# Moving the split weights of the 256-column products 64 bytes off a multiple of 256, in a fixed ring of four tiles

## The chip, the cores and the metric

The kernel runs on one core of one Trainium2 chip. The metric is the device time of one execution in microseconds, the median of three: 1817.12 us before the change (1815.8 to 1817.33). The profile is that of a further execution, which took 1815.54 us. TensorE (PE in the profile, its weight loads PEld) does the products, VectorE (DVE), ScalarE (ACT) and GpSimd (POOL) everything else, and SyncE (SP) issues most of the transfers.

## The reference

Two layers of a hybrid block on 512 tokens of 1024 features, in float32. What matters here are its matrix products:

```
h = rms_norm(x);  proj = h @ w_in            # 27 + 24 tiles of 128 columns, + two of 512
y_a = sparse attention (q, k, v, top 128 keys by an index score)
y_b = gated linear recurrence (conv, sigmoid gates, scan)
y_c = u * (w_spatial @ rms_norm(v))          # 8 masked 128x128 matrices
x = x + rms_norm(sum_n sigmoid(gate_n) * (y_n @ w_branch_n) @ w_out)
x = x + rms_norm(relu(rms_norm(x) @ w_up)**2 @ w_down)
x = x + rms_norm((p @ w_ple) * sigmoid(x @ w_ple_gate))
```

## The kernel before

Activations lie with features on the 128 partitions and the 512 tokens along the free dimension. TensorE works in `float32r`; to reach float32 precision every operand is split into a high part (rounded to `float32r`) and a low part (the rest), and each product is made of three: hi by hi, lo by hi, hi by lo (`mm3`, L361 to L363; the same three on one line in `gemm_arriving`, L419). The weight is the stationary operand, 128x128 at a time, and the activation streams past it: 512 columns as a rule, 256 where a stage is cut in two halves of the tokens so that the next norm can begin on the first half. The products of 256 columns are: in `gemm_halves`, the last three tiles of the output projection (`out` 5 to 7) and of the gate (`gate` 5 to 7); in `gemm_arriving`, the first four tiles of the up projection (`up` 0 to 3) and, in the second layer, the first three of the input projection (`xr` 0 to 2); and the spatial gating (`sp`), where the masked weight streams, two blocks of 128 columns at a time, past a stationary activation. The attention has small products of its own (transposes L1046, values L1060, logits L745 and L749), which use no weight.

Weights come in 306 tiles of 128x1024, in the order of a list (`order`). `prep` takes the next one: SP loads it into one of three buffers (`wr`), ACT casts it to the high part (`wh`, L253), DVE subtracts that from it for the low part (`wl`, L254). `getw` hands a weight out and first calls `prep` until it is three weights ahead (`LA`); for a branch weight (`br`) only one ahead. `wh` and `wl` are two tags of a pool with four buffers each (`NWB`). The built program shows which buffer each tile took: the four of a tag are not taken in turn, and each begins at a multiple of 512 bytes of its partition, as do the activations. A branch weight serves two branch products with a gate product between them (`gated`), so it is held longer than the gate weights that are handed out behind it.

[...] In the attention, `turn` transposes a piece of the probabilities into PSUM, splits it with a cast on ACT (L432) and a subtraction on DVE (L433), and `values` (L1060) multiplies both parts: four products, the first two with the high part, the other two with the low one.

Of the kernel before, what the change touches and what calls it, by code (L numbers as in the profile page):

```python
# [9 lines left out]
F32R = mybir.dt.float32r  # L10
# [35 lines left out]
def f32v(ap):  # L46
    return ap.bitcast(F32)
# [3 lines left out]
def hybrid_block_kernel(ctx, tc, xT, pT, pos, vec, bsp, freq, w_in, w_tok, w_lru, w_sp, w_br, w_out, w_up, w_dn, w_ple, w_gate, out, depth=DEPTH, dbg=None):  # L51
# [4 lines left out]
    wp = ctx.enter_context(tc.tile_pool(name="wp", bufs=1))  # L56
# [6 lines left out]
    def nm(p):  # L63
        uid[0] += 1
        return f"{p}_{uid[0]}"

    def tmp(dt=F32):
        return tp.tile([128, S], dt, tag="tmp", name=nm("tmp"), bufs=NTMP)
# [7 lines left out]
    def slot(tag, dt=F32, big=False):  # L76
        return cp.tile([128, 4, S] if big else [128, S], dt, tag=tag, name=nm(tag))
# [8 lines left out]
    NWB = 4  # L86
# [151 lines left out]
    nprep = [0]  # L238
    nget = [0]

    def prep():
        weights_first()
        i = nprep[0]
        nprep[0] += 1
        key, src = order[i]
        raw = wp.tile([128, 1024], F32, tag="wr", name=nm("wr"), bufs=3)
        nc.sync.dma_start(raw, src)
        if key[0] == "sp":
            r3 = raw.rearrange("p (g t) -> p g t", g=8)
            G.affine_select(out=r3, in_=r3, compare_op=ALU.is_ge, fill=0.0, base=0, pattern=[[0, 8], [1, 128]], channel_multiplier=-1)  # L250
        hi = wp.tile([128, 1024], F32R, tag="wh", name=nm("wh"), bufs=NWB)
        lo = wp.tile([128, 1024], F32R, tag="wl", name=nm("wl"), bufs=NWB)
        A.copy(hi, raw)  # L253
        V.tensor_sub(lo, raw, f32v(hi))  # L254
        prepared[key] = (hi, lo)
        if not strict[0]:
            return
        ins = nc.cur_bb.bb.instructions
        parts[:] = [len(ins)] + [next(i.name for i in reversed(ins) if i.engine == e) for e in ENG]
# [5 lines left out]
    def weights_first():  # L265

        if not parts:
            return
        for i in nc.cur_bb.bb.instructions[parts[0]:]:
            for e, name in zip(ENG, parts[1:]):  # L270
                if i.engine == e:
                    tc.add_manual_dep(i, name, mybir.DependencyInfo(mybir.DependencyClass.NoSync, mybir.DependencyReason.SCHED_ONLY), reason="weights first")
        parts.clear()

    def getw(key, ahead=LA):
        assert order[nget[0]][0] == key, (order[nget[0]][0], key)
        nget[0] += 1
        while nprep[0] < min(nget[0] + ahead, len(order)):
            prep()
        return prepared.pop(key)  # L280
# [104 lines left out]
    def gemm_halves(keys, xs, evac, done):  # L385


        ws = [getw(key, LA if i == 0 else 0) for i, key in enumerate(keys)]
        for r in HALVES:
            for i, w in enumerate(ws):  # L390
                ps = bank()[:, :S // 2]
                gemm(ps, w, xs, KT, r=r)
                evac(i, r, ps)
                if r is HALVES[1] and nprep[0] < len(order):
                    prep()
            done(r)

    def gemm_arriving(keys, xs, source, ranges, arrived=None, lag=LAG, tail=TAIL):


        n = len(keys)
        ws = [getw(key, 0) for key in keys[:-1]]
        pss = [bank() for _ in keys]
        last = {}
        for r in ranges:
            gen = source(r)
            for k in range(KT):
                with ordered(last):
                    next(gen)
                    todo = [(o, k) for o in range(len(ws))]  # L410
                    if len(ws) < n and k == lag:
                        ws.append(getw(keys[-1], 0))
                        todo += [(n - 1, q) for q in range(k + 1)]
                    if r is ranges[-1] and k >= KT - tail:
                        todo = [] if k < KT - 1 else [(o, q) for o in range(n) for q in range(KT - tail, KT)]
                    for i, (o, q) in enumerate(todo):
                        h3, l3 = [v.rearrange("p (k c) -> p k c", k=KT) for v in ws[o]]
                        for m in range(3):
                            PE.matmul(pss[o][:, r], (h3, l3, h3)[m][:, q], xs[q][m // 2][:, r], start=q == 0 and m == 0, stop=q == KT - 1 and m == 2)  # L419
                        if r is ranges[-1] and q == KT - 1 and o < n - 1:  # L420
                            prep()
                tick(0.65 * len(todo) * width(r) / S)
            if arrived is not None:
                arrived(r)
        while nprep[0] < nget[0] + LA:
            prep()
        return pss
# [146 lines left out]
    chunks = []  # L574
    for key, src in order[:3]:
        raw = wp.tile([128, 1024], F32, tag="wr", name=nm("wr"), bufs=3)
        hi = wp.tile([128, 1024], F32R, tag="wh", name=nm("wh"), bufs=NWB)
        lo = wp.tile([128, 1024], F32R, tag="wl", name=nm("wl"), bufs=NWB)
        prepared[key] = (hi, lo)
        chunks.append((src, raw, hi, lo))  # L580
    nprep[0] = 3
# [19 lines left out]
    for l in range(depth):  # L601
# [31 lines left out]
        def proj(name, ahead=LA):  # L633
            ps = bank()
            gemm(ps, getw(("in", l, name), ahead), XS, KT)
            return ps
# [12 lines left out]
        def rope(ps, n=128):  # L649
            t1, u = tmp(), tmp()  # L650
            V.tensor_mul(t1[:n], ps[:n], Cr[:n])
            V.stream_shuffle(u[:n], ps[:n], mask=SHUF)
            G.tensor_mul(u[:n], u[:n], Sr[:n])  # L653
            G.tensor_add(t1[:n], t1[:n], u[:n])  # L654
            return t1
# [25 lines left out]
        for j in range(4):  # L681
            ps = first[j]
            xr = tmp()
# [242 lines left out]
        for j in range(4):  # L926
# [7 lines left out]
            r, i = slot(f"B{j}"), tmp()  # L934
# [177 lines left out]
        for j in range(4):  # L1112
            f = rope(proj(f"q{j}"))
# [23 lines left out]
        for d in range(8):  # L1137
# [3 lines left out]
            hi, lo = slot(f"M{d}", F32R), ml[d // 4][:, d % 4]  # L1141
# [196 lines left out]
```

## Time and profile before

| what | value |
|---|---|
| median of three executions | 1817.12 us |
| the profiled execution | 1815.54 us |
| its span | 1813.8 us |
| PE busy | 1789.2 us, 99% |
| DVE, ACT, POOL busy | 63%, 43%, 19% |
| matmuls, each with its weight load | 8748 |

The span is what the profile covers; some 1.7 us of the execution lie around it. PE is busy from end to end at the full granted clock, so what a part costs is read from how far apart its matmuls start, and from the few places where PE waits. The busy time of one matmul row is longer than the distance to the next, because they overlap.

### The profile page before, as it was taken

What the parts mean: (1) busy time and instruction counts of PE and PEld (TensorE: products, weight loads), DVE (VectorE), ACT (ScalarE), POOL (GpSimd) and SP (SyncE); (2) the same over time, 40 slices, a digit from 0 to 9 for tenths busy, and PEclk for the clock granted to TensorE, in tenths of its full rate; (3) what the DMA queues carried; (4) which work ended last, traced back from release to release, by engine and by line L of the source; (5) the groups of instructions that cost most, each with busy time, mean ns of one, the idle gap of its engine ahead of it and who ended that gap; (6) DMA issues with size and microseconds to landing.
All of it is one profiled execution on the core that took longest, in us unless ns stands there. A gap on an engine that the chain in (4) does not pass through costs nothing.

```text
span 1813.8 us, 22748 instructions
## 1 busy us (share of the span) xinstructions
PE 1789.2 (99%) x8748; PEld 1497.5 (83%) x8748; DVE 1149.9 (63%) x1946; ACT 787.3 (43%) x1289; POOL 340.8 (19%) x277
## 2 busy tenths in 40 slices
PE   9999999999999999999999999999999999999997
PEld 7888788888988888888888888788889888888886
DVE  8789987656375254534688899876565743544345
ACT  6547246554443222223546473466534422222233
POOL 0612123200420000002454131332004100000033
PEclk9999999999999999999999999999999999999998
DMA  5312322222222232332222222322222323222321
GB/s 176 105 60 97 105 93 94 70 82 82 93 93 94 95 103 93 96 113 86 91 80 99 69 94 84 114 82 70 82 93 70 105 95 103 93 97 102 105 82 58
DMA packets 49676, 167.75 MB, mean 92 GB/s; under 512 B 6048, under 2 KB 8864, under 8 KB 49568
## 3 DMA queue, kind: packets, MB, share of 16 engines
q1 hardware_dynamic: 47376, 163.64, 27.3%
q10 hardware_dynamic: 2192, 2.67, 0.4%
q8 instruction: 68, 1.11, 0.3%
q14 instruction: 40, 0.33, 0.1%
HBM read 164.19 MB, written 2.10 MB: 92 GB/s over the span
## 4 chain that ended last, share of the span: by engine, by line
PE 75%; DVE 14%; POOL 4%; ACT 4%; issue 3%; DMA 0%; SPq 0%; POOLq 0%; ACTq 0%; DVEq 0%
PE ps L361 22%; PE ps L363 22%; PE ps L362 22%; PE ps L419 4%; DVE wl L254 3%; DVE tmp L794 2%; DVE m L792 2%; PE ps L668 2%; PE ps L1060 1%; POOL tmp L653 1%; ACT wh L253 1%; PE ps L1046 1%; POOL sacc L461 1%; PE ps L759 1%; POOL tmp L654 1%
## 5 line engine op out<-in xcount | busy, mean ns | idle before, releaser
L253 ACT CAST wh<-wr 128x1024 fp32r<-128x1024 f32 x303 | 317.2, 1050 | 476.9 <-PE ps L363 397.1
L254 DVE TENSOR_TENSOR wl<-wr,wh 128x1024 fp32r<-128x1024 f32 x303 | 379.2, 1254 | 199.7 <-ACT wh L253 199.3
L361 PE MATMUL ps<-xh,wh 128*128 128x512 f32 (+1 forms) x1296 | 502.5, 388 | 0.0
L363 PE MATMUL ps<-xl,wh 128*128 128x512 f32 (+1 forms) x1296 | 495.4, 382 | 0.0
L362 PE MATMUL ps<-xh,wl 128*128 128x512 f32 (+1 forms) x1296 | 495.2, 382 | 0.0
L363 PEld LDWEIGHTS ps<-xl,wh 128*128 128x128 f32 x1296 | 243.6, 188 | 47.7
L361 PEld LDWEIGHTS ps<-xh,wh 128*128 128x128 f32 x1296 | 243.8, 188 | 45.7 <-issue 1.9
L362 PEld LDWEIGHTS ps<-xh,wl 128*128 128x128 f32 x1296 | 244.1, 188 | 43.3
L461 POOL TENSOR_TENSOR sacc<-sacc,tmp 128x256 f32<-128x256 f32 (+1 forms) x92 | 98.0, 1065 | 884.6 <-issue 584.5
L363 PE MATMUL ps<-V,wh 128*128 128x512 f32 (+1 forms) x528 | 195.4, 370 | 0.0
L363 PE MATMUL ps<-B,wh 128*128 128x512 f32 x336 | 131.1, 390 | 0.0
L361 PE MATMUL ps<-A,wh 128*128 128x512 f32 x320 | 125.0, 390 | 0.0
L362 PE MATMUL ps<-A,wl 128*128 128x512 f32 x320 | 124.5, 389 | 0.0
L1197 DVE TENSOR_TENSOR M<-M,ps 128x512 f32<-128x512 f32 x48 | 33.0, 688 | 141.3 <-PE ps L363 141.3
L1185 DVE TENSOR_TENSOR tmp<-ps,R 128x512 f32<-128x512 f32 x64 | 43.8, 690 | 112.1 <-PE ps L363 109.5
L363 PEld LDWEIGHTS ps<-V,wh 128*128 128x128 f32 x528 | 99.5, 188 | 16.8
L361 PE MATMUL ps<-K,wh 128*128 128x512 f32 x256 | 99.6, 389 | 0.0
L362 PE MATMUL ps<-K,wl 128*128 128x512 f32 x256 | 99.6, 389 | 0.0
L419 PE MATMUL ps<-xl,wh 128*128 128x256 f32 (+1 forms) x264 | 86.2, 326 | 5.5 <-DVE xl L567 5.1
L419 PE MATMUL ps<-xh,wl 128*128 128x256 f32 (+1 forms) x264 | 84.1, 319 | 0.8 <-DVE wl L254 0.8
L419 PE MATMUL ps<-xh,wh 128*128 128x256 f32 (+1 forms) x264 | 84.5, 320 | 0.1
L363 PEld LDWEIGHTS ps<-B,wh 128*128 128x128 f32 x336 | 63.1, 188 | 13.4
(243 smaller groups left out, 2835.7 us busy)
## 6 DMA issues: line engine op xcount, KB each, us to landing
wr<-in_w_in_dram SPq DMA_DIRECT2D x95, 512.0 KB, 3.3
wr<-in_w_up_dram SPq DMA_DIRECT2D x64, 512.0 KB, 3.2
wr<-in_w_dn_dram SPq DMA_DIRECT2D x64, 512.0 KB, 3.2
wr<-in_w_br_dram SPq DMA_DIRECT2D x24, 512.0 KB, 3.2
wr<-in_w_tok_dram SPq DMA_DIRECT2D x16, 512.0 KB, 3.2
wr<-in_w_out_dram SPq DMA_DIRECT2D x16, 512.0 KB, 3.2
wr<-in_w_gate_dram SPq DMA_DIRECT2D x16, 512.0 KB, 3.2
X<-in_xT_dram SPq DMA_DIRECT2D x8, 256.0 KB, 5.7
```

What stands on the lines that cost most here:

```text
L253: A.copy(hi, raw)
L254: V.tensor_sub(lo, raw, f32v(hi))
L361: PE.matmul(ps, wh, xh, start=start, stop=False)
L362: PE.matmul(ps, wl, xh, start=False, stop=False)
L363: PE.matmul(ps, wh, xl, start=False, stop=stop)
L419: PE.matmul(pss[o][:, r], (h3, l3, h3)[m][:, q], xs[q][m // 2][:, r], start=q == 0 and m == 0, stop=q == KT - 1 and m == 2)
L461: G.tensor_add(sacc[:, r], sacc[:, r], self.q[r.start, r.stop])
L668: PE.matmul(ps, x, w, start=k == 0 and i == 0, stop=k == KT - 1 and i == 2)
L792: V.max(m8, (sc if r == 0 else wk)[:, :n])
L794: V.match_replace(wk[:, :n], m8, (sc if r == 0 else wk)[:, :n], -3.0e38)
L1185: V.tensor_mul(t, ps, R)
L1197: V.tensor_add(F[d], F[d], ps)
```

## The change

`home` takes the place of the two pool tags. There are four tiles with a tag each (`wp0` to `wp3`), taken strictly in turn as weights are recorded, and each holds hi and lo of one weight side by side. The two odd tiles are 2064 elements wide and the even ones 2096, so that in the built program the even ones begin at a multiple of 256 bytes and the odd ones at 192 more. The offset `c` of 16 elements (64 bytes) is set so that the weights named in `narrow` begin 64 or 192 bytes past a multiple of 256 and all others at a multiple of 256 (for two of the four tiles one that is not a multiple of 512). The work arrays behind them lie 512 bytes further on.

```
+    narrow = set()
+    for l in range(depth):
+        narrow.add(("sp", l))
+        narrow.update(("out", l, d) for d in (5, 6, 7))
+        narrow.update(("gate", l, d) for d in (5, 6, 7))
+        narrow.update(("up", l, 0, i) for i in range(4))
+        if l:
+            narrow.update(("in", l, f"xr{j}") for j in range(3))
+    ring = [0]
+
+    def home(key):
+
+        i = ring[0] % NWB
+        ring[0] += 1
+        t = wp.tile([128, 2064 if i % 2 else 2096], F32R, tag=f"wp{i}", name=nm("wp"))
+        c = 16 if (key in narrow) == (i % 2 == 0) else 0
+        return t[:, c:c + 1024], t[:, c + 1024:c + 2048]
...
-        hi = wp.tile([128, 1024], F32R, tag="wh", name=nm("wh"), bufs=NWB)
-        lo = wp.tile([128, 1024], F32R, tag="wl", name=nm("wl"), bufs=NWB)
+        hi, lo = home(key)
         A.copy(hi, raw)
         V.tensor_sub(lo, raw, f32v(hi))
```

The same two lines are replaced where the first three weights are set up. No instruction is removed, and none is added but six loads of an activation table on ACT, three in each layer, where the scheduler sets square roots (L957) and gates' tanh (L919) in turns; SP's loads keep their order. Lines of the kernel after are 17 or 18 higher than before.

What moves is shown at one place, a piece of the first head pair's attention whose values are multiplied while a branch product runs (layer 0). The same is found at a second place of the layer, in the next head pair, and at the same two in layer 1. On ACT before, the cast of the probabilities (`tmp_3092`, L432) stands between the casts of two weights:

```order
L432 CAST tmp_3056<-ps_3051 128x512
L253 CAST wh_3078<-wr_3076 128x1024
L432 CAST tmp_3092<-ps_3088 128x384
L253 CAST wh_3186<-wr_3184 128x1024
L1033 ACTIVATE tmp_3111,mx_3112<-tmp_3111,mx_3112 128x128
```

On ACT after, both weights' casts stand ahead of it (`tmp_3035` is the same piece; `wp_3129` is the branch weight, recorded last, and `wp_3022` the gate weight recorded before it):

```order
L450 CAST tmp_3001<-ps_2996 128x512
L271 CAST wp_3129<-wr_3127 128x1024
L271 CAST wp_3022<-wr_3020 128x1024
L450 CAST tmp_3035<-ps_3031 128x384
L1050 ACTIVATE tmp_3054,mx_3055<-tmp_3054,mx_3055 128x128
```

The two weights have changed places, and the probabilities have moved behind the second. DVE's two subtractions moved likewise, ahead of that of the probabilities (`tmp_3036`). On PE before, at the same place, the values with the high part (`tmp_3092`) stand five products ahead of the branch product's end, those with the low part (`tmp_3093`) at its end:

```order
L361 MATMUL ps_3168<-B_417_1976,wh_2850 128x512
L1060 MATMUL ps_2988<-tmp_3092,V_455_2139 128x256
L1060 MATMUL ps_2988<-tmp_3092,V_455_2139 128x128
L362 MATMUL ps_3168<-B_417_1976,wl_2851 128x512
L363 MATMUL ps_3168<-B_418_1977,wh_2850 128x512
L361 MATMUL ps_3168<-B_428_2038,wh_2850 128x512
L362 MATMUL ps_3168<-B_428_2038,wl_2851 128x512
L363 MATMUL ps_3168<-B_429_2039,wh_2850 128x512
L1060 MATMUL ps_2988<-tmp_3093,V_455_2139 128x256
L1060 MATMUL ps_2988<-tmp_3093,V_455_2139 128x128
L361 MATMUL ps_3183<-xh_12_187,wh_2978 128x512
```

On PE after, all four stand behind the branch product (`ps_3111`), whose weight is `wp_2798`:

```order
L380 MATMUL ps_3111<-B_382_1941,wp_2798 128x512
L381 MATMUL ps_3111<-B_383_1942,wp_2798 128x512
L379 MATMUL ps_3111<-B_392_2002,wp_2798 128x512
L380 MATMUL ps_3111<-B_392_2002,wp_2798 128x512
L381 MATMUL ps_3111<-B_393_2003,wp_2798 128x512
L1077 MATMUL ps_2933<-tmp_3035,V_417_2101 128x256
L1077 MATMUL ps_2933<-tmp_3035,V_417_2101 128x128
L1077 MATMUL ps_2933<-tmp_3036,V_417_2101 128x256
L1077 MATMUL ps_2933<-tmp_3036,V_417_2101 128x128
L379 MATMUL ps_3126<-xh_12_187,wp_2924 128x512
```

The five products that stood between the two pairs of values have moved ahead of both.

## Rows read from the trace of the kernel before

**Rows 1.** The page: busy us (share) xinstructions; granted TensorE clock in 40 slices.
```profile
PE 1789.2 (99%) x8748; PEld 1497.5 (83%) x8748; DVE 1149.9 (63%) x1946; ACT 787.3 (43%) x1289; POOL 340.8 (19%) x277
PEclk9999999999999999999999999999999999999998
```

**Rows 2.** Timeline of PE, out projection of 512 columns: start us, length us.
```profile
451.74 0.39 PE L363 MATMUL ps<-V,wh 128*128 128x512 f32 x1
...
461.94 0.39 PE L363 MATMUL ps<-V,wh 128*128 128x512 f32 x1
```

**Rows 3.** The same a little later, in its halves of 256 columns.
```profile
471.36 0.28 PE L361 MATMUL ps<-M,wh 128*128 128x256 f32 x1
...
477.96 0.28 PE L362 MATMUL ps<-M,wl 128*128 128x256 f32 x1
```

**Rows 4.** Groups of PE by shape, products of 256 columns: count, busy us, mean ns.
```profile
L419 PE MATMUL ps<-xh,wh 128*128 128x256 f32 x176 | 50.2, 285 | 0.0
...
L361 PE MATMUL ps<-M,wh 128*128 128x256 f32 x96 | 27.5, 286 | 0.0
...
L361 PE MATMUL ps<-wh,K 128*128 128x256 f32 x32 | 9.0, 282 | 0.0
```

**Rows 5.** Timeline of PE: four transposes, eight products of 2 columns.
```profile
271.59 0.60 PE L1046 MATMUL ps<-ident,tmp 128*128 128x128 f32 x4
...
845.72 1.05 PE L471 MATMUL ps<-ones,tmp 128*128 128x2 f32 x8
```

**Rows 6.** Groups of PE and PEld by shape: the same kinds, mean ns of one.
```profile
L1046 PE MATMUL ps<-ident,tmp 128*128 128x128 f32 x160 | 26.0, 273 | 0.0
...
L471 PE MATMUL ps<-ones,tmp 128*128 128x2 f32 x24 | 3.3, 254 | 1.5 <-ACT tmp L455 1.5
...
L362 PEld LDWEIGHTS ps<-xh,wl 128*128 128x128 f32 x1296 | 244.1, 188 | 43.3
...
L1046 PEld LDWEIGHTS ps<-ident,tmp 128*128 128x128 f32 x160 | 20.4, 140 | 7.0 <-ACT tmp L1035 0.8
...
L471 PEld LDWEIGHTS ps<-ones,tmp 128*128 128x128 f32 x24 | 3.0, 191 | 2.2 <-ACT tmp L455 2.2
```

**Rows 7.** Waits of PE and of PEld: us in total, times, longest.
```profile
PE ps L419 <- DVE xl L567: 5.1, 10, 0.9
...
PEld ps L1060 <- ACT tmp L432: 1.2, 4, 0.4
```

**Rows 8.** Timeline of ACT at the two places of moved instructions, layer 0.
```profile
328.74 1.05 ACT L253 CAST wh<-wr 128x1024 fp32r<-128x1024 f32 x1 [7.27 <-PE ps L363]
329.69 0.47 ACT L432 CAST tmp<-ps 128x384 fp32r<-128x384 f32 x1
331.90 1.05 ACT L253 CAST wh<-wr 128x1024 fp32r<-128x1024 f32 x1 [1.74 <-PE ps L363]
...
362.02 1.05 ACT L253 CAST wh<-wr 128x1024 fp32r<-128x1024 f32 x1 [5.68 <-PE ps L363]
...
367.64 1.05 ACT L253 CAST wh<-wr 128x1024 fp32r<-128x1024 f32 x1 [0.98 <-PE ps L363]
```

**Rows 9.** Timeline of PE at the first of them: a branch product's end.
```profile
331.47 0.39 PE L363 MATMUL ps<-B,wh 128*128 128x512 f32 x1
331.70 0.34 PE L1060 MATMUL ps<-tmp,V 128*128 128x256 f32 x2
```

**Rows 10.** Timeline of DVE at the first.
```profile
329.82 1.23 DVE L254 TENSOR_TENSOR wl<-wr,wh 128x1024 fp32r<-128x1024 f32 x1 [6.74 <-ACT wh L253]
330.97 0.55 DVE L433 TENSOR_TENSOR tmp<-ps,tmp 128x384 fp32r<-128x384 f32 x1
```

**Rows 11.** Windows of all engines: the recurrence in layer 0, two stages of arriving halves.
```profile
150.00:215.00 65.00, 64.91 (x287) 53.45 (x286) 61.39 (x126) 34.04 (x48) 18.29 (x16) 1.00 0.26 87
...
479.00:511.00 32.00, 30.80 (x252) 30.09 (x250) 24.07 (x46) 18.10 (x43) 20.82 (x25) 1.00 0.15 50
```

**Rows 12.** Groups of ACT, 150 to 215 us.
```profile
L957 ACT ACT_TABLE_LOAD x1 | 1.3, 1283 | 0.0
```

## The prediction before the run

> **What bounds the kernel now.** I read the page first. TensorE is busy 99% of the span and its granted clock is full from end to end, while VectorE stands at 63% and ScalarE at 43% [rows 1]. So the time is the sum of TensorE's matmuls plus a few places where it waits; an edit counts only if it changes how far apart matmuls start, or how long TensorE stands. I therefore went to TensorE's timeline and took the distances from start to start, in stretches without a wait. The reader is to see two paces. In the out projection, 45 products of 512 columns start between 451.74 and 461.94, which is 10.20/45 = 226.7 ns each [rows 2]. In its halves, 55 products of 256 columns lie between 471.36 and 477.96, which is 6.60/55 = 120.0 ns [rows 3]. The difference, 106.7 ns, is what 256 columns cost; twice that is 213.3, so either kind pays 13.3 ns beyond its columns. The groups by shape gave the counts, the waits what TensorE stands for, and the timelines of ScalarE, TensorE and VectorE around 330 us the margins at the place where the order changes. The windows by stage came last.
>
> **The change, part 1: where the weights lie.** Narrow products with weights number 3 x 176 = 528 in the arriving halves, 3 x 96 x 2 = 576 in the halves of the projections (xh stands for the gate there and M for out, 96 each), and 3 x 32 = 96 in the spatial gating [rows 4]. What 64 bytes do to one of them no row shows, since all weights here begin at multiples of 512 bytes, so I bound the saving s per product. From above: the columns alone, 106.7 ns, s = 13.3. From below: the pace could lose as much as it now pays, 133.3 ns, s = -13.3; nothing excludes that, for another address can also be a worse one. [...] Eight products of 2 columns take 1.05 us in all and one takes 0.254, so they start (1.05 - 0.254)/7 = 114 ns apart; their weight loads last 191 ns as the rows have it, those of the wide products 188 [rows 5, 6]. Four transposes of 128 columns start (0.60 - 0.273)/3 = 109 ns apart, with a shorter weight load, 140 ns [rows 5, 6]. That suggests a floor of 109 to 114 ns set by the weight load, under which a narrow product doesn't come. I take 113, near the first, because its loads are the ones of this kind: s = 7, in a range of 4 to 10.
>
> [...]
>
> The sum: 576 x 7 = 4.0 us in the halves and 96 x 7 = 0.7 in the gating, where the weight streams instead of standing. Of the 528 arriving products I count three quarters, 2.8 us. There TensorE also waits for VectorE's low parts, 5.1 us in ten waits [rows 7], and the stretch has 30.80 of 32 us busy [rows 11]: a product that ends earlier there partly waits longer. Together -7.5 us.
>
> The wide weights are to stay as they were, but two of the four tiles now begin at odd multiples of 256 bytes. There are about 6,900 wide products; 1 ns on half of them would be 3.4 us either way. No row shows such an address; I take nothing and keep 3.4 us for the range.
>
> **Part 2: the order.** In the strict ring a gate weight needs the tile that the running branch product still reads, while the branch weight recorded after it takes the tile that came free earlier. Before, the pool gave these two in the other order. So ScalarE's second cast now starts only when the branch product has ended, and the cast of the probabilities, which stood between, comes behind it. That second cast began at 331.90 in the trace, 0.43 us after the start of the branch product's last matmul at 331.47 [rows 8, 9]. The next instruction on ScalarE starts 0.95 us after a weight's cast does (329.69 - 328.74), and the cast of the probabilities takes 0.47 [rows 8]: it ends at 331.90 + 0.95 + 0.47 = 333.32. TensorE has its values next, before the gate product whose weight is long ready, and could start them at 331.70 [rows 9]. With some 0.06 us to get going it stands about 1.68 us. The two values run 0.2 to 0.3 us, then the low parts are wanted. On VectorE the weight's subtraction comes first, and the next instruction follows 1.15 us after its start (330.97 - 329.82), then the low part takes 0.55 [rows 10]. From the end of the weight's cast, 332.95, this makes 332.95 + 1.15 + 0.55 = 334.65, plus about 0.06; less 333.38, where the first pair starts, and 0.2 for that pair, about 1.07 us more. So one place costs 2.75 us. Behind the stalled values on TensorE stands the whole gate product, so nothing fills the hole.
>
> The second place, in the next head pair, has the same shape: casts of two weights at 362.02 and 367.64, the second again right after the branch product, with probabilities between them [rows 8]; after the change both weights come first. I give it the same price; with two places in each of two layers that is 4 x 2.75 = 11.0 us. The small waits of the values for the cast that stand there now, 1.2 us in four [rows 7], are part of the same spots and go: +9.8 us net. What could hide some of it is the work between: a product wider apart on TensorE, or a cast that starts earlier than I read; if one place of the two in a layer is covered, 4.9 us remain.
>
> **Part 3: the rest.** Six table loads on ScalarE at 1.3 us are 7.7 us, three in the recurrence of each layer [rows 12]. They are covered: ScalarE is busy 34.04 of 65 us there. VectorE, at 61.39 of 65, is the engine that would notice [rows 11], and if each load delayed it in full the cost would be 7.7 us; TensorE has other products to run in that stretch and was busy 64.91 of 65, so I take nothing. With hi and lo in one tile, a new weight waits for the last reader of both, which is at most one product later; three weights ahead are 24 wide products each, 5.4 us, and hide it. SP's order of loads is the same.
>
> **Sum.** 9.8 - 7.5 = +2.3 us on the profiled execution of 1815.54, which is 1817.8. The median of the runs lies 1.6 us above that execution, so the forecast is 1819.4 us.
>
> **Rivals.** First (slower): the address of the weights changes nothing, and the order is paid alone. For it: both paces pay the same 13.3 ns, as if it belonged to each product and not to where its weight lies; that the 2-column products need 114 ns with the same kind of weight load shows only that a load has a length. Time: 1815.54 + 9.8 + 1.6 = 1826.9, from 1822 (one place covered) to 1829. It decides if s is below 4. [...]
>
> Second (faster): the pace comes down to 109 or 106.7 ns, s = 11 to 13.3, over the same 576 + 96 + 396 = 1,068 products: 11.7 to 14.2 us. With the order at 9.8 or half covered at 4.9 that is -1.9 to -9.3 us, 1808 to 1815 with the 1.6. For it: the halves run with no wait at all between TensorE's products, so every ns there is kept. Against it: the 114 ns of the products that stream almost nothing.
>
> Third: 64 bytes off is the worse address, s = -13.3: 14.2 us lost on top of the order, 1841. For it: every pace in the rows was measured with weights at multiples of 512, so that may be the good place. Against it: the 13.3 ns that even these pay. No row tells the two apart, and it keeps a small chance.
>
> **How the numbers follow.** Forecast 0.38, first rival 0.30, second 0.25, third 0.07. The measurement can tell about 0.2%, 3.6 us, so "same" is 1813.5 to 1820.8. The likeliest case with s from 4 to 10 spans 1816 to 1823: 0.28 of it is same, 0.10 slower. The first rival gives 0.29 slower, 0.01 same; the second 0.18 faster, 0.07 same; the third 0.07 slower. Together: faster 0.18, same 0.36, slower 0.46. The range 1810 to 1829 leaves out the third rival and the lower part of the second, and holds the 3.4 us of the wide tiles.
>
> **What the profile after would show.** Right: in the halves of the out projection narrow products about 113 ns apart, wide ones still 226.7; on ScalarE two weights' casts in a row ahead of that of the probabilities; among TensorE's waits four of the values for that cast, near 1.7 us, and four for the low part, near 1.1. Six more table loads with no new wait of TensorE beside them. Wrong: a pace of 120 (first rival), 109 or less (second), over 120 (third), a wide pace that moved, or values that still stand between products and wait for nothing.

## The result, and the profile after

The kernel after takes 1834.55 us (median of four, 1830.27 to 1838.17), the kernel before 1817.22: a ratio of 1.0098, 95% interval 1.0083 to 1.0112, 17.3 us slower. 1819.4 in a range of 1810 to 1829 was predicted. The profiled execution took 1836.37 with a span of 1834.6, 20.8 us over that of before; the account below is of this one.

The page, beside [rows 1]:

```profile
PE 1796.7 (98%) x8748; PEld 1499.1 (82%) x8748; DVE 1153.8 (63%) x1946; ACT 797.4 (43%) x1295; POOL 339.4 (18%) x277
PEclk9999999999999999999999999999999999999999
```

The same counts (six more on ACT, the table loads), and at this grain a clock that looks full. TensorE's waits (total, times, longest) already show where time went; beside [rows 7] the lines of L1077 with waits of this length are new, and so are those of L380 and L379:

```profile
PE ps L437 <- DVE xl L585: 6.3, 10, 0.9
PE ps L1077 <- ACT tmp L450: 6.0, 4, 1.5
PE ps L1077 <- DVE tmp L451: 3.6, 4, 0.9
PE ps L380 <- DVE wp L272: 2.5, 1, 2.5
...
PE ps L685 <- DVE wp L272: 1.8, 2, 1.2
...
PE ps L379 <- ACT wp L271: 0.8, 1, 0.8
```

L1077 is the values (L1060 before): four holes of 1.5 and four of 0.9 us, 9.6 together. (The line of L437 answers to L419 in [rows 7], 5.1 there.) The first place on ScalarE, answering to [rows 8]:

```profile
332.10 1.05 ACT L271 CAST wp<-wr 128x1024 fp32r<-128x1024 f32 x1 [7.26 <-PE ps L381]
334.82 1.04 ACT L271 CAST wp<-wr 128x1024 fp32r<-128x1024 f32 x1 [1.66 <-PE ps L381]
335.77 0.47 ACT L450 CAST tmp<-ps 128x384 fp32r<-128x384 f32 x1
```

and on TensorE, answering to [rows 9], with what comes behind it:

```profile
334.39 0.39 PE L381 MATMUL ps<-B,wp 128*128 128x512 f32 x1
336.30 0.45 PE L1077 MATMUL ps<-tmp,V 128*128 128x256 f32 x2 [1.51 <-ACT tmp L450]
337.64 0.45 PE L1077 MATMUL ps<-tmp,V 128*128 128x256 f32 x2 [0.90 <-DVE tmp L451]
...
339.86 0.63 PE L379 MATMUL ps<-xh,wp 128*128 128x512 f32 x1
340.29 0.63 PE L380 MATMUL ps<-xh,wp 128*128 128x512 f32 x1
340.71 0.63 PE L381 MATMUL ps<-xl,wp 128*128 128x512 f32 x1
...
342.77 0.39 PE L379 MATMUL ps<-xh,wp 128*128 128x512 f32 x1
343.01 0.40 PE L380 MATMUL ps<-xh,wp 128*128 128x512 f32 x1
```

The second cast begins 0.43 us after the branch product's last start, the probabilities' cast follows it, TensorE stands twice. Then comes what the prediction doesn't have: from 339 to 342.5 us the same 512-column products start 0.43 us apart, not 0.23. Windows of TensorE over the holes (length, busy, granted clock) say why:

```profile
162.00:167.00 5.00, 1.75 (x7) 1.00 0.00 1
339.00:343.00 4.00, 4.00 (x14) 0.57 0.20 78
376.00:384.00 8.00, 7.88 (x25) 0.57 0.21 68
1171.00:1176.00 5.00, 4.56 (x13) 0.66 0.26 85
1245.00:1250.00 5.00, 2.58 (x13) 1.00 0.62 199
1284.00:1292.00 8.00, 7.14 (x22) 0.57 0.18 66
```

The granted clock fell from full to half (0.50 in every window of 1 us that lies inside a fall) after three of the four holes, and once after a wait of 1.4 us at 1171 us; the mean of 0.57 over 4 us is 3.4 us at half, in which 1.7 us of work is lost. Over the four stretches that is (3.4 + 6.8 + 3.4 + 6.8)/2 = 10.2 us. One hole of the same length, at 1246 us, left the clock alone. Slices of 46 us hide all this. The mean granted clock of each execution shows it without a trace: 0.991 to 0.994 in the four of the kernel after, the slowest at the lowest, and 0.995 to 0.998 in the 51 of the kernel before that were timed beside the experiments.

A fifth hole lies in the recurrence of layer 0, where the prediction saw cover:

```profile
162.45 0.39 PE L381 MATMUL ps<-V,wp 128*128 128x512 f32 x1
163.60 0.50 PE L379 MATMUL ps<-xh,wp 128*128 128x512 f32 x1 [0.76 <-ACT wp L271]
166.59 0.50 PE L380 MATMUL ps<-xh,wp 128*128 128x512 f32 x1 [2.49 <-DVE wp L272]
```

A branch product ends and the next gate product's weight is not there: 3.3 us. The order on ScalarE, with the built program's names, shows the same exchange as at the other places, the branch weight cast first (at 150.99) and the gate weight recorded ahead of it second (at 162.52), behind the recurrence's own activations.

The built program has this exchange at more places than the four of the prediction: 19 pairs of neighbouring weights, nine in layer 0 and ten in layer 1, are cast in the other order. TensorE stands at five of them. At 300.15 us, for example, a second cast comes late and probabilities' casts stand behind it in the same way, but TensorE has seven products of the gate product ahead of the values and does not wait.

And the narrow products did get faster. TensorE in the output projection's halves, answering to [rows 3]:

```profile
484.27 0.28 PE L379 MATMUL ps<-M,wp 128*128 128x256 f32 x1
...
488.87 0.28 PE L379 MATMUL ps<-M,wp 128*128 128x256 f32 x1
...
494.12 0.28 PE L380 MATMUL ps<-M,wp 128*128 128x256 f32 x1
...
494.91 0.28 PE L381 MATMUL ps<-V,wp 128*128 128x256 f32 x1
```

The first 39 distances are (488.87 - 484.27)/39 = 118 ns each, and towards the end seven take 0.79 us, 113 ns each; 120 before. By the built program the first 24 products shown and those at the end use the same weight at the same address, for the first half of the tokens and for the second: its place alone does not set the pace.

The account of the 20.8 us: four holes 9.6, the fifth 3.3, half clock 10.2, narrow products of the halves and the gating -2.8 (their distances from start to start add up to 81.8 us before and 79.0 after). That is 20.3; the rest is small waits of both signs.

### The profile page after: what moved, and what is told of

Read it like the earlier page. It is cut to its first block, busy times and chain, and to the rows that moved or that the text cites. A ratio compares the mean times of both kernels' runs of the same rounds, so it can differ in the third digit from the quotient of the medians.

```text
span 1834.6 us, 22736 instructions
## 1 busy us (share of the span) xinstructions
PE 1796.7 (98%) x8748; PEld 1499.1 (82%) x8748; DVE 1153.8 (63%) x1946; ACT 797.4 (43%) x1295; POOL 339.4 (18%) x277
## 4 chain that ended last, share of the span: by engine, by line
PE 77%; DVE 14%; POOL 3%; issue 3%; ACT 2%; DMA 1%; SPq 0%; ACTq 0%; POOLq 0%; DVEq 0%
PE ps L379 22%; PE ps L381 22%; PE ps L380 22%; PE ps L437 3%; PE ps L685 3%; DVE wp L272 3%; DVE tmp L811 2%; DVE m L809 2%; PE ps L1077 1%; PE ps L1063 1%; POOL sacc L479 1%; DVE tmp L888 1%; PE ps L776 1%; POOL X L565 1%; ACT wp L271 1%
## 5 line engine op out<-in xcount | busy, mean ns | idle before, releaser
L271 ACT CAST wp<-wr 128x1024 fp32r<-128x1024 f32 x303 | 316.8, 1050 | 501.3 <-PE ps L381 422.7
L272 DVE TENSOR_TENSOR wp<-wr,wp 128x1024 fp32r<-128x1024 f32 x303 | 377.4, 1249 | 216.7 <-ACT wp L271 216.3
L379 PE MATMUL ps<-xh,wp 128*128 128x512 f32 (+1 forms) x1296 | 503.8, 389 | 0.8 <-ACT wp L271 0.8
L380 PE MATMUL ps<-xh,wp 128*128 128x512 f32 (+1 forms) x1296 | 496.5, 383 | 2.6 <-DVE wp L272 2.5
L381 PE MATMUL ps<-xl,wp 128*128 128x512 f32 (+1 forms) x1296 | 496.4, 383 | 0.0
L381 PEld LDWEIGHTS ps<-xl,wp 128*128 128x128 f32 x1296 | 244.4, 189 | 48.1
L380 PEld LDWEIGHTS ps<-xh,wp 128*128 128x128 f32 x1296 | 244.7, 189 | 47.2 <-DVE wp L272 3.6
L379 PEld LDWEIGHTS ps<-xh,wp 128*128 128x128 f32 x1296 | 244.4, 189 | 46.7 <-issue 1.9
L381 PE MATMUL ps<-V,wp 128*128 128x512 f32 (+1 forms) x528 | 194.9, 369 | 0.0
L381 PE MATMUL ps<-B,wp 128*128 128x512 f32 x336 | 130.9, 390 | 0.0
L379 PE MATMUL ps<-A,wp 128*128 128x512 f32 x320 | 125.0, 391 | 0.0
L380 PE MATMUL ps<-A,wp 128*128 128x512 f32 x320 | 124.5, 389 | 0.0
L437 PE MATMUL ps<-xh,wp 128*128 128x256 f32 (+1 forms) x528 | 117.9, 317 | 0.9 <-DVE wp L272 0.6
L379 PE MATMUL ps<-K,wp 128*128 128x512 f32 x256 | 99.6, 389 | 0.0
L380 PE MATMUL ps<-K,wp 128*128 128x512 f32 x256 | 99.6, 389 | 0.0
L437 PEld LDWEIGHTS ps<-xh,wp 128*128 128x128 f32 x528 | 86.5, 188 | 8.7 <-ACT xh L575 0.8
L437 PE MATMUL ps<-xl,wp 128*128 128x256 f32 (+1 forms) x264 | 85.7, 325 | 6.8 <-DVE xl L585 6.3
L685 PE MATMUL ps<-wp,xh 128*128 128x512 f32 x256 | 81.0, 391 | 1.8 <-DVE wp L272 1.8
```

The costliest lines, as they stand in the source:

```text
L379: PE.matmul(ps, wh, xh, start=start, stop=False)
L380: PE.matmul(ps, wl, xh, start=False, stop=False)
L381: PE.matmul(ps, wh, xl, start=False, stop=stop)
L685: PE.matmul(ps, x, w, start=k == 0 and i == 0, stop=k == KT - 1 and i == 2)
```

## The experiments

Theory A, formed after the result: the exchange of gate and branch weights makes the holes, the clock behind them doubles their price, and the offset gains a little. Its main rival, B: the addresses themselves cost it. Each kernel was timed beside the kernel before on the same chip; its median there is given where it matters.

**The ring without the offset.**

```
+    narrow.clear()
     ring = [0]
```

> The ring and the order of the kernel after, but no weight is offset: all begin at multiples of 256 bytes. Theory A (the order makes the hole, the half clock behind it makes it dearer, the offset gains a little): narrow products 120 ns apart again, TensorE's values wait 1.5 and 0.9 us at four places, stretches of granted clock 0.5 behind some of them, and the time is that of the kernel after plus 3 to 4 us, 1836 to 1840, with the spread of the kernel after. Rival B (the offset itself, or the tiles' new addresses under the casts and subtractions, costs the 17 us): without the offset the time falls back to 1817 to 1822.

1838.41 us, ratio 1.0119 (1.0106 to 1.0133), 3.9 us over the kernel after: inside A's range, though the two intervals overlap and the 3.9 us are hardly clear of noise. B, 17 us lower, falls. The waits are those of the kernel after:

```profile
PE ps L1078 <- ACT tmp L451: 6.1, 4, 1.5
PE ps L438 <- DVE xl L586: 4.7, 9, 0.9
PE ps L1078 <- DVE tmp L452: 3.6, 4, 0.9
PE ps L381 <- DVE wp L273: 2.5, 1, 2.5
```

and in this profile all five holes have a fall of the clock behind them, each of 3.4 us at half:

```profile
167.00:171.00 4.00, 4.00 (x12) 0.57 0.60 185
337.00:342.00 5.00, 4.12 (x14) 0.66 0.39 133
378.00:383.00 5.00, 5.00 (x19) 0.66 0.10 41
1245.00:1250.00 5.00, 4.10 (x14) 0.66 0.42 146
1286.00:1291.00 5.00, 5.00 (x18) 0.66 0.13 50
```

**The offset in the order of before.** The tile of each weight comes from a list of 306 numbers, taken from a pool of four joint tiles.

```
-        i = ring[0] % NWB
+        i = SLOTS[ring[0]]
```

> The same tiles and offsets as the kernel after, but each weight's tile is taken from a fixed list, the sequence in which a pool of four tiles with hi and lo together hands them out; with it the instructions stand in the order of the kernel before on TensorE, SyncE and GpSimd, and nearly so on ScalarE and VectorE. Theory A: no hole, no half clock before the last 10 us, narrow products 114 ns apart; 672 of them by 6 ns are 4.0 us, less disturbances, so 1812.5 to 1815, below the kernel before. Rival B: the loss stays with the addresses, 1830 or more. Rival C (the arriving halves give their gain back to VectorE, and the rest is lost too): 1816 to 1818.

1815.04 us against 1815.81 for the kernel before, ratio 0.9996 (0.9987 to 1.0004). B is out: same tiles, same offsets, 19.5 us less. But the gain of A, 1 to 3 us, is not resolved either; C comes nearest. No wait of the values is left, narrow products are 113 to 118 ns apart and wide ones stay at 227 at odd multiples of 256 as well as at even ones. Two things eat the gain. The arriving products give theirs back: their starts add up to 74.0 us, 74.2 before, while VectorE's low parts keep them waiting (5.9 us, [rows 7] 5.1). And a wait for a weight's low part is new, the last line:

```profile
PE ps L442 <- DVE xl L590: 5.9, 9, 0.9
PE ps L690 <- DVE wp L277: 3.4, 4, 1.8
PE ps L385 <- DVE wp L277: 1.9, 2, 1.0
```

**Every weight offset.**

```
-        c = 16 if (key in narrow) == (i % 2 == 0) else 0
+        c = 16 if i % 2 == 0 else 0
```

> As the previous kernel, but every weight lies 64 or 192 bytes off a multiple of 256, the wide products' too. Theory A (the offset shortens something in the weight load, which only a product of 256 columns feels): wide products stay 226.7 ns apart, time as the previous kernel within 2 us. Rival D (the 13.3 ns on top of either size come from where the weight lies): wide products come closer by some 6 ns, 6,900 of them, 35 to 45 us faster. Rival E (the offset is bad for wide products, which is why they are left where they were): wide products further apart, at 1 ns 7 us slower, at 7 ns 45 us slower.

1836.68 us, ratio 1.0112 (1.0096 to 1.0127), with no hole and a full clock until the last 8 us: rival E, some 3 ns on each of the wide products, and A's "wide products don't feel it" is wrong. In a stretch without waits:

```profile
648.17 0.39 PE L386 MATMUL ps<-xl,wp 128*128 128x512 f32 x1
...
650.04 0.39 PE L385 MATMUL ps<-xh,wp 128*128 128x512 f32 x1
```

Eight distances in 1.87 us, 234 ns each. What helps a narrow product (113 to 118 ns for 120) hurts a wide one (234 for 227).

**A table of offsets.**

```
+        if key in narrow or steady:
+            c = ((16, 0, 8, 4, 12) if i % 2 else (0, 8, 16, 24, 32, 40, 48, 4, 12))[turn % (5 if i % 2 else 9)]
```

> As the planned kernel, but narrow weights, and wide ones of the up and down projections, cycle through offsets of 0, 16, 32, 48, 64, 96, 128, 160, 192, 208, 224 and 240 bytes past a multiple of 256. One look, for a table of pace by offset from one trace. Theory A1 (any place off a multiple of 256 serves): 114 ns everywhere but at 0. Theory A2 (only 64 bytes off a multiple of 128, so 64 and 192): 114 there, 120 elsewhere. Theory A3 (places off a multiple of 64 are worse): over 120 at 16, 48, 208, 240. For wide products all theories but D and E say 226.7 at every offset. The time is no test; 1813 to 1820.

One execution, 1828.43 us. Median distance from start to start, by the bytes that the weight lies past a multiple of 256 (narrow between narrow, wide between wide; 44 products or more in each; where two numbers stand, the multiple is an even and an odd one):

```
bytes    0        16       32       48       64       96   128   160  192      208  224       240
narrow   120,120           117,117  117      114,114  119  120   118  118,117  117  117       118
wide     227,227  227,230  233,233  234,233  233,233  234  232   232  230,229  233  234,234   228,227
```

A1 and A3 fall. A2 holds in part: 64 bytes is best and 128 no better than none, but 192 gives 118 and the places between 117 to 119. Since one address ran at both 118 and 113 ns in the kernel after, differences of a few ns between the narrow columns are not due to the address alone. For wide products a multiple of 256 is best and 16 bytes to either side nearly as good. Why the two sizes answer in opposite ways none of these runs tells.

**High parts alone, in the kernel before.** Hi and lo stay in tiles of their own; every engine has the order of the kernel before.

```
+        lo = wp.tile([128, 1024], F32R, tag="wl", name=nm("wl"), bufs=NWB)
+        hi = wp.tile([128, 1072 if i % 2 else 1040], F32R, tag=f"wh{i}", name=nm("wh"))
+        c = (0 if i % 2 else 16) if key in narrow else (48 if i % 2 else 0)
```

> The kernel before, instruction for instruction in its order on every engine, hi and lo in tiles of their own as there; only the high parts of the narrow weights lie 64 bytes off a multiple of 256, all else at multiples of 256. Theory A: products with hi (two of three) start 114 ns apart, those with lo 120; in the halves and the gating 448 products by 6 ns are 2.7 us, less some disturbance: 1813 to 1814.5 beside 1815.8 for the kernel before, and none of the 1.9 us of waits of L385 for the low part that the planned kernel showed. Rival C (the gain is lost again whatever the order): 1815.5 to 1816.

1814.75 against 1816.52 us, ratio 0.9994 (0.9986 to 1.0003): by the medians a gain of 1.8 us, by the ratio 1.1, where A asked for 1.3 to 2.8, and not resolved. The pace was not as expected: all three kinds of narrow product are 118 ns apart, those with the aligned low part too, and the starts in halves and gating add up to 80.6 us (81.8 before), half of the 2.7 us. The wait for the low part of the joint tile is gone. This profile also has a fall of the clock, 3.4 us at half from 909.6 us on, though no weights are exchanged here:

```profile
909.00:914.00 5.00, 4.77 (x28) 0.66 0.01 3
```

The waits ahead of it, 0.85 us at 906.88 and 0.72 at 909.23, stand in the kernel before as well, there at full clock.

**The ring, with the probabilities free of the weights.**

```
         for i in nc.cur_bb.bb.instructions[parts[0]:]:
+            if i.name in free:
+                continue
```

`free` holds the cast and the subtraction that `turn` records; the loop, in `weights_first`, binds all else on ScalarE and VectorE to stand behind the weight recorded before it.

> The kernel after with its strict ring and offsets; only the cast and the subtraction of the probabilities in the attention are freed from the rule that weights come first, so that at the four places they stand ahead of the second weight's cast again. Theory A (the hole comes from the probabilities queued behind a cast that waits for the branch product): no wait of the values of 1.5 and 0.9 us, no half clock in the attention, 11 to 17 us less than the kernel after, 1818 to 1824; what stays is the hole of 3.3 us in the recurrence of layer 0. Rival F (the strict ring is short of a tile there, and TensorE waits for a weight in any case): the wait moves to a product for its weight's cast, and the time stays above 1830.

1827.64 us, ratio 1.0059 (1.0043 to 1.0074): seven less than the kernel after, short of the 11 that A asked for, and below what F said. The values still wait for their cast four times, 4.0 us in all. At the first place the hole at the branch product's end is gone, but seven us later another piece waits (first line); the second place has a hole of another kind:

```profile
342.69 0.45 PE L1082 MATMUL ps<-tmp,V 128*128 128x256 f32 x2 [0.97 <-ACT tmp L453]
...
373.30 0.44 PE L1082 MATMUL ps<-tmp,V 128*128 128x256 f32 x2 [1.04 <-ACT tmp L453]
...
374.78 0.50 PE L382 MATMUL ps<-xh,wp 128*128 128x512 f32 x1 [1.04 <-DVE tmp L938]
```

At the second place ScalarE still casts the weight first (371.82) and the probabilities second (372.77): the freed cast could go ahead, and in the built program it does not; why, no run shows. Four falls of the clock stay, one of them behind the hole in the recurrence. So the rule that weights come first is part of the cause, not all of it.

**A joint tile without offset.**

```
+        t = wp.tile([128, 2048], F32R, tag="wp", name=nm("wp"), bufs=NWB)
+        c = 0
```

> The kernel before with hi and lo side by side in one tile of a pool of four, no offset: TensorE's order is that of before. Theory A (what the planned kernel gained in its narrow products, it partly lost because a new weight's cast must wait for the last reader of both halves): 1817 to 1819, 1.5 to 3 us slower than the kernel before, with waits of products for their low part that the kernel before doesn't have. Rival G (the joint tile is free): 1815 to 1816.5.

1817.02 against 1816.52 us, ratio 1.0004 (0.9995 to 1.0013): between A and G, within either's reach of the interval. The wait is there (products for the low part, 2.2 us in three, none in the high-parts kernel). Against this control the planned kernel's offset would be worth 0.08%, 1.5 us, which is less than either interval: not resolved.

**One exchange, and four.** In the planned list two tiles change names from one weight on, so that a gate weight and the branch weight behind it change places. Later weights keep their order and take the tile of the new name; instructions move at the exchanged places alone.

```
-    20132103...    (SLOTS from the 57th weight on; for four exchanges
+    02130123...     the same at the 62nd, 210th and 215th)
```

> The planned kernel (order of before, offsets of after) with one pair of tiles exchanged: at the first head pair of layer 0 the gate weight and the branch weight recorded behind it change places, as the strict ring has them; everything else keeps its order. Theory A: one hole, the values waiting 1.5 us for the cast and 0.9 for the low part, 2.9 us with the restart, and behind it either 3.4 us at half the granted clock (1.7 us lost) or not: 2.9 to 4.6 us over the planned kernel, 1818 to 1820. Rival H (the hole alone is harmless, and the loss is in how the whole ring shifts the prefetch): within 1.5 us of the planned kernel, 1814.5 to 1816.5.

> The same with all four places exchanged, two in each layer. The kernel after has besides these the later weights in the recurrence of layer 0 and the table loads. Theory A: four times the price of one, 11.6 us with no half clock up to 18.4 with it behind every hole: 1826.5 to 1833.5. What then remains to the kernel after, 1834.55, is the hole in the recurrence, 3.3 to 5 us. Rival H: 1815 to 1820.

One: 1817.73 us, ratio 1.0011 (1.0002 to 1.0020), which is 0.15%, 2.7 us, over the planned kernel's ratio. Of its eleven runs five lie within 1816.97 to 1817.31, at a mean granted clock of 0.996 or 0.997, the others from 1817.73 to 1821.54, the three slowest at 0.995. The profiled one, 1821.54, has the clock down for 6.8 us behind the hole, and for 3.4 at 70 us, behind a wait of 1.79 us for a low part that the planned kernel also has (1.82), there at full clock:

```profile
70.00:75.00 5.00, 5.00 (x16) 0.66 0.31 105
330.00:337.00 7.00, 5.21 (x23) 1.00 0.23 64
337.00:344.00 7.00, 6.37 (x18) 0.51 0.24 86
```

The 2.7 us fall just short of A's 2.9 to 4.6, and with intervals of 0.09% this kernel alone does not exclude H; the fastest runs may be a hole without a fall, but no trace of one was taken. Four: 1833.23 us, ratio 1.0094 (1.0078 to 1.0109), at the upper end of A; H is out. The waits are 6.0 and 3.6 us again, and the clock is at half behind all four:

```profile
335.00:340.00 5.00, 4.09 (x16) 0.66 0.41 145
...
376.00:381.00 5.00, 5.00 (x19) 0.66 0.10 38
...
1240.00:1245.00 5.00, 2.71 (x11) 0.85 0.64 206
1245.00:1250.00 5.00, 5.00 (x23) 0.81 0.03 7
...
1281.00:1289.00 8.00, 7.78 (x25) 0.57 0.20 66
```

By 5 x 0.34, 5 x 0.34, 5 x 0.15 + 5 x 0.19 and 8 x 0.43 that is 8.5 us of work lost; with the 9.6 it makes 18.1, and by the ratios the kernel is 0.98%, 17.8 us, over the planned one. The exchange at these four places accounts for nearly the whole loss; the offsets follow the planned kernel's rule. The kernel after lies only 1.3 us higher, not 3.3 to 5, and the profiles show what offsets its fifth hole of 3.3 us: the four-exchange kernel keeps the planned kernel's waits for low parts, 3.4 us in L690 and 1.9 in L385, where the kernel after has 1.8 (L685) and none.

## Why the prediction was wrong

From the +2.3 us of the sum to the 20.8 of the profile it is 10.2 us of half clock, 3.3 of the fifth hole, 4.7 of gain that did not come (2.8 for 7.5), less 0.2 where the four holes took 9.6 for 9.8; 0.5 us are small waits.

- **The step that failed: "So one place costs 2.75 us."** It priced a hole at its length. With the half clock behind it, a place cost 2.4 to 5.8 us in the profiles, and the four together 17.8. The first rival, without such a term, ended at 1829, right only in its sign; with the 8.5 us of the four-exchange kernel and a gain of 1.5 the sum would have come near the time: 1815.54 + 1.6 + 9.8 + 8.5 - 1.5 = 1833.9. The view for it was there: the last slice of the clock in [rows 1] is not full, though the prediction reads it as full from end to end. The fall behind that digit came in the kernel before, right after the wait of 1.5 us of L471 [rows 6]:

```profile
1803.00:1813.00 10.00, 1.29 (x6) 0.54 0.42 146
```

- **The second: "three weights ahead ... hide it."** It was not hidden where two weights change places: the exchange that I had found beside the attention happens in the recurrence too, where no probabilities stand between, and TensorE waits for the weight itself. I had looked for it only where the values moved. And where each weight keeps its turn, products still wait for the joint tile's low part, 1.9 us in the planned kernel and 2.2 without the offset.
- **The offset.** The 113 ns taken from products that stream almost nothing came out as a number: 113 to 118 ns. That the weight load sets such a floor no run shows; they show the pace change with the weight's address, and one address at 118 and at 113. The gain was too high: 2.8 us in halves and gating instead of 4.7, because each stretch starts at 118 and because the gating, where the weight streams, only went from 119 to 118; and nothing of the 2.8 in the arriving products, where TensorE waits for VectorE's low parts (5.9 us in the planned kernel, 5.1 before). Of the 7.5 us, the two pairs of kernels that differ in the offset alone show 1.5 (planned against joint tile) and 3.9 (kernel after against the ring without offset), the first inside the noise and the second hardly outside it. The wide products at odd multiples of 256 cost nothing, as taken: 227 ns at either.
- **The first rival's address.** That the address of the weights changes nothing, the table of offsets contradicts: a narrow product is 114 ns apart at 64 bytes and 120 at a multiple of 256, a wide one 233 and 227.
- **The order.** The mechanism, its four places and its size were right: 1.51 and 0.90 us where 1.68 and 1.07 stood. (By its own terms the second is 334.65 + 0.06 - 333.38 - 0.2 = 1.13.)
- **The table loads and SP's order** cost nothing that a wait shows, as said; in layer 0 the added loads stand behind 172 us, after the fifth hole.

## What to carry to other kernels

On a kernel that TensorE bounds, a hole can be dearer than its length (2.4 us of waiting cost up to 5.8 a place here): look at the granted clock in windows of a few microseconds behind each wait, and price a new wait with what it may take down. When tiles out of a pool become a strict ring, follow for each weight which one frees its tile; one that is held longer makes later weights change places, at every stage that has one and not only where you saw it, and see at each whether the engine has other work ahead of what will wait. An alignment that suits one product size can spoil another (64 bytes off: 114 for 120 ns at 256 columns, 233 for 227 at 512): apply it by size, and check the rows of both.

## What the runs showed of the hardware

TensorE's pace depends on where the stationary operand lies, in opposite ways for 256 and 512 columns: 120 ns at multiples of 256 bytes and 113 to 118 at 64 or 192 past one, against 227 and 229 to 234. The place is not all: one weight at one address ran at 118 ns and, 8 us later, at 113. Offsetting the high parts alone, two loads of three, gave 118 ns throughout, where the aligned low parts had 120 before, so that a product's distance hangs on its neighbours' weights too.

The granted clock did not fall behind every hole: equal waits (1.51 and 0.90 us) were followed by full clock, by 3.4 us or by 6.8 us at half of it, and one of 1.8 us by a fall in one profile and none in four others. What decides between these stays open. That the fall comes with the hole is shown by the counts: behind the 13 holes of this form in four profiles it fell 12 times, while of six profiles without an exchange five have full clock until the last 12 us. The sixth, the high-parts kernel, fell once behind waits of 0.85 and 0.72 us, with none longer in the 11 us ahead of it. A kernel with the hole filled by other work was not run.
